# Scaling the output weights a tile ahead, moving the last token tile's transposes and first gather forward, and interleaving the two halves of the last expert unit

## The chip, the cores and the metric

One core of a Trainium2 chip runs the whole kernel. The metric is device microseconds (us) of one execution. Engines are named as the profile names them: PE (TensorE, the matrix engine; PEld is its weight load), DVE (VectorE), ACT (ScalarE), POOL (GpSimd) and SP (SyncE, which issues most DMAs here). Each engine works through its own instructions strictly in the order in which the kernel issues them, and waits on semaphores for the others.

## The reference

One decoder layer over 512 tokens of width 1024, in float32. What matters here:

```python
merged = sigmoid(mg_h) * (o_h @ w_br_hg) + sigmoid(mg_n) * (o_n @ w_br_nsa)
y = (1 + g1) * (merged @ w_out)                 # g1: one scale per output column
x = layer_norm(ALPHA * x + y) * ln1_g + ln1_b
h = layer_norm(x) * (1 + sc2) + sh2
# hierarchical MoE: top group of 4, top 2 of its 8 experts, SwiGLU experts of width 512
y = (1 + g2) * sum over 2 experts of  weight * ((silu(h @ w1) * (h @ w3)) @ w2)
x = layer_norm(ALPHA * x + y) * ln2_g + ln2_b
```

The kernel's units cover all 32 experts whatever the routing, so all of `exp_w1`, `exp_w3` and `exp_w2` is read.

## The kernel before

Tokens lie in NT = 4 tiles of 128. A float32 product is made of three faster ones: an operand is split into a rounded part (`wh`, ACT, L274) and the rest (`wl`, DVE, L275), and three matmuls of the fp32r type are summed. SBUF holds a pool Q of 36 buffers of 128x1024 and a pool S of 24 of 128x512, PSUM a pool of 8 banks. A buffer that is asked for again waits until the last reader of its former content is done.

**Projections.** `Block` holds one block of weight columns: `fetch1` loads a tile of it, `split1` splits a tile. `run_jobs` goes through a list of jobs; after every few matmuls a job yields, and `ahead` then splits one more tile of the blocks to come: first those of the next block, then those of blocks marked `early`. Only the two blocks `wo` (the halves of `w_out`, four tiles of 128x1024 each) are early, and for these `split1` first multiplies the tile by 1 + g1 on DVE (L273). So for each `wo` tile the order is: L273 on DVE, `wh` on ACT, `wl` on DVE. These eight tiles are split during the last jobs of the branch projections (`br_job` with MGN, PSUM tile `pbr`), between DVE's own work of those jobs (L1084, L1088, ACT L1090, DVE L1091: gate, add, and split of the merged rows) and the plain splits of the next branch block (two tiles per block, L274 and L275).

**Output projection, layer norm, routing.** For each token tile i, `out_piece` multiplies the merged rows by `wo` (PSUM `pyo`) and adds x into `z`; `ln` then does the layer norm, the router's logits, the choice of experts, and the row's place within its expert. Tiles 0 to 2 are woven into the matmuls of the next tile; for the last tile `ln` runs by itself. In it DVE makes the statistics and the norm (L1198 to L1205) while PE transposes z (`tail_logits`, PSUM `pzT`; ACT copies it to `zT`) and multiplies it by the router's weights (`plg`, twice: L187, L1218). DVE then chooses the experts (L1223 to L1253, which ends in the mask `mb`), PE runs `gather_first([0, 1])` (a one-hot gather of the rows of tiles 0 and 1 that go to the first four experts, into four banks `pgx`, 32 matmuls), then counts earlier tokens with `mb` (`prk`, L1260 to L1262), then `gather_first([2])`. DVE turns the counts into slots and a one-hot (L1266 to L1275) and splits the last tile (L1277). `gather_first([3])` ends the gather, L1354 and L1356 write it to `xe`, and the first expert unit begins (PSUM `p`).

**Expert units.** 13 units of 128 token slots follow, for 2, 1, 2 or 4 experts at a time; `up` makes the SwiGLU (PSUM `p`), `down` the product with `exp_w2` (`py`) and `combine` adds its rows to the tokens (`pcb`, L1561). With four experts each has 32 slots and its matmuls use 32 of PE's 128 columns, so four run side by side. `load_unit` issues the weights on SP (L1306) in tiles of 512 KB, always as soon as a Q buffer comes free.

**The last unit** is written out (L1671 to L1770). `half_up(h)` makes one half of the output columns, `weighted_halves` scales and splits it (`y`, `yh`, `yl`), `half_add` adds the rows of one token tile (`pcb`, L1707, with their sums), `squares` (ACT, L1689) sums squares about the first half's mean `nsh` (L1721). The rows of `ln2_g` and `ln2_b` are spread over the partitions by 8 matmuls (`pl2`, in the profile `pl`, L1727) and four ACT copies (L1728). Order before: half 0 on PE, `y`; then the split of the two `ln2` rows (L1714 to L1718); the four `half_add`; `nsh`; the 8 `pl2` with their copies; the four `squares`; half 1 on PE; `y` of half 1; the loop for overflow (no block here, but its control flow), then the adds of half 1, the statistics and the output. The weights of half 1 are the last eight tiles that SP loads (L1303).

Of the kernel before, what the change touches and what calls it, by code (L numbers as in the profile page):

```python
# [26 lines left out]
AF = mybir.ActivationFunctionType  # L27
OP = mybir.AluOpType
# [3 lines left out]
NT = T // 128  # L32
# [107 lines left out]
def hybrid_kernel(ctx, tc, a, out, dbg=None, stop=None):  # L140
# [20 lines left out]
    def PS(name):  # L161
        return pp.tile([128, 512], F32, name=name, tag="ps", bufs=8)
# [61 lines left out]
    def layer_stats(src, pre, st=None, later=False):  # L224
        if st is None:
            st = small(pre + "st", 12)
            for q in range(2):
                V.bn_stats(st[:, q * 6:(q + 1) * 6], src[:, q * 512:(q + 1) * 512])
        mv = small(pre + "mv", 2, bufs=4 if pre == "l0" else 2)
        V.bn_aggr(mv, st.rearrange("p (q s) -> p q s", s=6))  # L230
        rs = small(pre + "rs", 2, bufs=4 if pre == "l0" else 2)
        A.activation(rs[:, 0:1], mv[:, 1:2], AF.Ln, bias=eps[:, 0:1])
        A.activation(rs[:, 0:1], rs[:, 0:1], AF.Exp, scale=-0.5)
        if not later:
            V.scalar_tensor_tensor(rs[:, 1:2], mv[:, 0:1], -1.0, rs[:, 0:1], op0=OP.mult, op1=OP.mult)
        return mv, rs
# [13 lines left out]
    class Block:  # L250
        def __init__(self, view, c0, n=256, kt=KT, raw=False, early=False):
            self.view, self.c0, self.n, self.kt, self.raw, self.early = view, c0, n, kt, raw, early
            self.kp = {128: 8, 256: 4, 280: 2, 512: 2}[n]
            self.np = kt // self.kp
            self.w, self.h, self.l = [], [], []

        def fetch1(self):
            kp, n, j = self.kp, self.n, len(self.w)
# [4 lines left out]
        def fetch(self):  # L263
            while len(self.w) < self.np:
                self.fetch1()

        def split1(self, sub=None):
            kp, n, j = self.kp, self.n, len(self.h)
            wh = Q("wh", F32R)[:, :kp * n].rearrange("p (k n) -> p k n", k=kp)
            wl = Q("wl", F32R)[:, :kp * n].rearrange("p (k n) -> p k n", k=kp)  # L270
            if self.early:

                V.tensor_mul(self.w[j], self.w[j], g1b[:, None, self.c0:self.c0 + n].to_broadcast([128, kp, n]))  # L273
            A.activation(wh, self.w[j], AF.Copy)  # L274
            (sub or V).tensor_sub(wl, self.w[j], wh.bitcast(F32))  # L275
            self.h.append(wh)
            self.l.append(wl)
# [30 lines left out]
    g1b = None  # L308
# [313 lines left out]
    for f in range(4):  # L622
        t = S("kcT")
# [535 lines left out]
    def gather_first(tiles, ks=range(8)):  # L1159


        if not pgx0:
            pgx0.extend(PS("pgx").rearrange("p (k s) -> p k s", k=2) for _ in range(4))
        end = tiles[-1] == NT - 1
        for part in ((xhh,), (xhl,)) if end else ((xhh, xhl),):
            for k in ks:
                for i in tiles:
                    for x in part:
                        mm(pgx0[k // 2][:, k % 2, :], x[i][:, k * 128:(k + 1) * 128], hots0[i // 2][:, i % 2, :],
                           i == 0 and x is xhh and k % 2 == 0, end and x is xhl and k % 2 == 1)  # L1170
# [21 lines left out]

    def ln(i, z, st):
        last = i == NT - 1
        mv, rs = layer_stats(z, "l1", st, later=True)
        ac = Q("acc")
        acc.append(ac)
        V.scalar_tensor_tensor(ac, z, mv[:, 0:1], l1g, op0=OP.subtract, op1=OP.mult)  # L1198
        if last:
            plg, lgT = tail_logits()  # L1200
        st = small("l2st", 12)
        for half in range(2):
            s_ = slice(half * 512, (half + 1) * 512)
# [48 lines left out]
        V.scalar_tensor_tensor(mb[:, i, :], iota[:, 0:32], ef[:, 1, i:i + 1], oh2[:, 0, i, :], op0=OP.is_equal, op1=OP.add)  # L1252
        V.tensor_scalar(oh2[:, 1, i, :], iota[:, 0:32], ef[:, 1, i:i + 1], None, op0=OP.is_equal)  # L1253
        if last:
            gather_first([0, 1])
        else:
            yield LN_R

# [74 lines left out]

    W.drain()

    def tail_logits():
        i = NT - 1
        zT[i] = []
        for k4 in range(2):
            pt = z_transposed(i, zs[i], k4 * 4, 4)  # L1340
            t = S("zT")
            A.activation(t, pt, AF.Copy)
            zT[i].append(t)
        return logits_of(i)
    for _ in ln(NT - 1, zs[NT - 1], l1st[NT - 1]):
        pass
    load_unit((0, 1), 8, 12, w_first)
# [340 lines left out]
    def squares(i, h):  # L1688
        A.activation(sq, acc[i][:, halves_[h]], AF.Square, bias=nsh[:, i:i + 1], accum_out=sqs[:, i, h:h + 1])  # L1689

    def half_up(h):

        py = PS("py")
        m = 128 // len(w_now["exp_w2"])
        for k in range(4):
            for x, w in enumerate(w_now["exp_w2"]):
                mm(py[m * x:m * x + m, :], aT[:, k, m * x:m * x + m], w[2 * h + k // 2][:, k % 2 * 512:k % 2 * 512 + 512],
                   k == 0, k == 3, pos=(0, m * x) if m < 128 else None)
        return py

    def half_add(h, y, i):

# [4 lines left out]
        V.tensor_tensor_reduce(out=z, in0=z, in1=pc_, scale=1.0, scalar=0.0, op0=OP.add, op1=OP.add,  # L1707
                               accum_out=sums[:, i, h:h + 1])

    py = half_up(0)  # L1710
    y = weighted_halves(py, cs_, 0, 512)

    oner = Q("oner", F32R)[0:1, 0:128]
    A.activation(oner, ones[0:1, :], AF.Copy)  # L1714
# [1 line left out]
    for t, h_, l_ in zip(l2r, l2h, l2l):  # L1716
        A.activation(h_, t, AF.Copy)
        V.tensor_sub(l_, t, h_.bitcast(F32))  # L1718
    for i in range(NT):
        half_add(0, y, i)  # L1720
    V.tensor_scalar(nsh, sums[:, :, 0], -1.0 / 512, None, op0=OP.mult)  # L1721
    l2g, l2b = Q("l2g"), Q("l2b")
    for t, h_, l_ in zip((l2g, l2b), l2h, l2l):
        for s_ in halves_:
            ps = PS("pl2")
            for j, x in enumerate((h_, l_)):
                mm(ps, oner, x[:, s_], j == 0, j == 1)  # L1727
            A.activation(t[:, s_], ps, AF.Copy)  # L1728
    for i in range(NT):
        squares(i, 0)  # L1730
    py = half_up(1)
    y = weighted_halves(py, cs_, 512, 512)
    overflow()
    A.preload_act_table_set("natural_log_exp_and_others")
    for i in range(NT):
# [61 lines left out]
```

## Time and profile before

| | us |
|---|---|
| median of 3 runs | 1262.7 (1262.7, 1264.41, 1262.7) |
| the profiled execution | 1262.44 |
| its span, first to last instruction | 1260.7 |
| mean granted TensorE clock | 0.978 |
| busy: PE / DVE / ACT / POOL | 1174.7 / 691.6 / 431.3 / 82.8 |
| HBM read | 292.73 MB |

The span is 1.74 us shorter than the execution's time. Busy shares are averages over stages that differ: through the first 600 us PE is busy without a break, from 770 us on the DMA engines are. So what a part of the change is worth is read in its own stage: the branch projections (620 to 690 us), the last tile's routing (744 to 764 us) and the last unit (1222 us to the end).

### The profile page before, as it was taken

How to read it: one execution, taken by the hardware profiler on the slowest of the kernel's cores; microseconds unless marked ns; L12 is line 12 of the kernel's file. 1: busy time of each engine (PE TensorE's matmuls, PEld its weight loads, DVE VectorE, ACT ScalarE, POOL GpSimd, SP SyncE). 2: the span in 40 equal slices, each digit the busy share in tenths (PEclk: the TensorE clock that was granted, in tenths of full speed). 3: DMA queues.
4: the chain of work that ended last, by engine and by line, in shares of the span. 5: the costliest groups of instructions: out<-in, count | busy, mean ns of one | idle time of the engine just before them, and what ended most of it. 6: DMA issues, size and time to landing. Idle time of an engine off the chain costs nothing. (4 is left out here: it accounts for less than half of the span.)

```text
span 1260.7 us, 18162 instructions
## 1 busy us (share of the span) xinstructions
PE 1174.7 (93%) x6455; PEld 805.9 (64%) x6455; DVE 691.6 (55%) x1626; ACT 431.3 (34%) x904; POOL 82.8 (7%) x164
## 2 busy tenths in 40 slices
PE   5999999999999999999987979999999899999976
PEld 4788898778888888878765764434436235455322
DVE  5564988777566656323575687634235124445314
ACT  4333666664445363554232242200102002122014
POOL 3011111101101011002000020000000000000000
PEclk8999999999999999999998989999999999999997
DMA  9954323224234243326334189999999999999991
GB/s 325 299 145 150 106 66 119 85 95 144 88 126 122 75 151 117 100 92 198 105 113 147 54 292 340 409 409 409 408 409 409 409 409 408 406 406 403 409 366 71
DMA packets 137629, 296.10 MB, mean 235 GB/s; under 512 B 11195, under 2 KB 74883, under 8 KB 137536
## 3 DMA queue, kind: packets, MB, share of 16 engines
q1 hardware_dynamic: 128224, 268.57, 58.1%
q0 software_dynamic: 8544, 23.97, 6.1%
q10 hardware_dynamic: 768, 2.37, 0.6%
q8 instruction: 52, 0.85, 0.3%
q14 instruction: 41, 0.34, 0.1%
HBM read 292.73 MB, written 4.76 MB: 236 GB/s over the span
## 5 line engine op out<-in xcount | busy, mean ns | idle before, releaser
L182 PE MATMUL p<-ew,xe 128*32 128x512 f32 (+1 forms) x960 | 195.4, 597 | 11.4 <-DMA ew<-in_exp_w_dram 11.0
L275 DVE TENSOR_TENSOR wl<-wst,wh 128x1024 fp32r<-128x1024 f32 (+1 forms) x93 | 109.5, 1200 | 84.5 <-ACT wh L274 83.8
L182 PEld LDWEIGHTS p<-ew,xe 128*32 128x32 f32 (+1 forms) x960 | 53.2, 122 | 146.9 <-issue 83.1
L274 ACT ACTIVATE wh<-wst 128x1024 fp32r<-128x1024 f32 (+1 forms) x94 | 93.6, 1031 | 44.8 <-DVE wst L273 32.1
L1512 DVE TENSOR_TENSOR s<-s,p 128x512 f32<-128x512 f32 x13 | 8.9, 688 | 176.6 <-PE p L182 160.9
L182 PE MATMUL py<-ew,aT 128*32 128x512 f32 (+1 forms) x464 | 96.4, 598 | 8.7 <-DMA ew<-in_exp_w_dram 5.8
L182 PEld LDWEIGHTS py<-ew,aT 128*32 128x32 f32 (+1 forms) x464 | 24.7, 121 | 73.2 <-issue 36.5
L1520 ACT ACTIVATE aT<-pat 128x512 f32<-128x512 f32 x13 | 7.8, 597 | 177.4 <-PE pat L186 177.4
L1561 DVE TENSOR_TENSOR acc<-acc,pcb 128x512 f32<-128x512 f32 x96 | 58.3, 678 | 7.9 <-PE pcb L180 7.9
L1535 ACT ACTIVATE yh<-y 128x512 fp32r<-128x512 f32 x26 | 16.4, 630 | 132.3 <-DVE y L1533 130.8
L180 PE MATMUL pgx<-pm,xhh 128*128 128x256 f32 (+1 forms) x224 | 56.3, 295 | 0.0
L180 PE MATMUL pgx<-pm,xhl 128*128 128x256 f32 (+1 forms) x224 | 55.0, 290 | 0.0
L1533 DVE SCALAR_TENSOR_TENSOR y<-py,cs,g2b 128x512 f32<-128x512 f32 x26 | 19.4, 748 | 62.2 <-PE py L182 62.0
L180 PE MATMUL pmg<-hh,wh 128*128 128x512 f32 x128 | 50.4, 394 | 0.0
L180 PE MATMUL psg<-hh,wh 128*128 128x512 f32 x128 | 50.3, 393 | 0.0
L180 PE MATMUL psg<-hl,wh 128*128 128x512 f32 x128 | 49.9, 390 | 0.0
L180 PE MATMUL psg<-hh,wl 128*128 128x512 f32 x128 | 49.9, 390 | 0.0
L180 PE MATMUL pmg<-hh,wl 128*128 128x512 f32 x128 | 49.8, 389 | 0.0
L180 PE MATMUL pmg<-hl,wh 128*128 128x512 f32 x128 | 49.8, 389 | 0.0
L180 PE MATMUL pcb<-yh,pT 128*128 128x512 f32 x104 | 43.6, 420 | 6.6 <-issue 5.1
L513 POOL DMA_DIRECT2D adaw<-in_ada_w_dram x64 | 34.6, 542 | 196.5 <-PE ptp L186 44.8
L180 PEld LDWEIGHTS pgx<-pm,xhh 128*128 128x128 f32 x224 | 44.2, 200 | 3.2 <-issue 2.3
(538 smaller groups left out, 2788.1 us busy)
## 6 DMA issues: line engine op xcount, KB each, us to landing
ew<-in_exp_w_dram SPq DMA_DIRECT2D x380, 512.0 KB, 10.1
wst<-in_w_in_dram SPq DMA_DIRECT2D x66, 512.0 KB, 4.9
adaw<-in_ada_w_dram POOLq DMA_DIRECT2D x64, 256.0 KB, 3.1
adaw<-in_ada_w_dram SPq DMA_DIRECT2D x16, 512.0 KB, 9.2
wst<-in_w_br_hg_dram SPq DMA_DIRECT2D x8, 512.0 KB, 5.5
wst<-in_w_br_nsa_dram SPq DMA_DIRECT2D x8, 512.0 KB, 3.6
wst<-in_w_out_dram SPq DMA_DIRECT2D x8, 512.0 KB, 6.5
ext_d<-ext_d POOLq DMA_DIRECT2D x1, 2560.0 KB, 17.2
```

Source lines behind the costliest of these rows:

```text
L180: PE.matmul(o, l, r, start=start, stop=stop)
L182: PE.matmul(o, l, r, start=start, stop=stop, tile_position=pos)
L274: A.activation(wh, self.w[j], AF.Copy)
L275: (sub or V).tensor_sub(wl, self.w[j], wh.bitcast(F32))
L513: P_.dma_start(w, ada[:, k, 2048 + j * 512:2560 + j * 512])
L1512: V.tensor_mul(s1, s1, p3)
L1520: A.activation(aT, at_.rearrange("p (f s) -> p f s", f=4), AF.Copy)
L1533: V.scalar_tensor_tensor(y, py, cs_, g2b[c0 // 512][:, c0 % 512:c0 % 512 + n], op0=OP.mult, op1=OP.mult)
L1535: A.activation(yh, y, AF.Copy)
L1561: V.tensor_add(acc[i][:, s_], acc[i][:, s_], pc_)
```

## The change

Three edits. (1) `Block.scale(j)` is the former multiplication by 1 + g1; `split1` for tile j issues it for tile j + 1 too, between `wh` on ACT and `wl` on DVE. It does so only for tiles that have been fetched, and all four of a block are. (2) In `ln` of the last tile, the transposes and copies of z (`tail_transposed`) and `gather_first([0])` are issued first; the logits follow where they were, and after the choice of experts only `gather_first([1])` runs before the counts. (3) In the last unit, the split of the `ln2` rows comes ahead of half 0; the 8 `pl2` matmuls follow half 0 on PE at once, their copies follow the first `yh` on ACT; then the first inner index of half 1 is issued expert by expert, each of the four matmuls followed by one `half_add` of half 0; then the second index, `nsh`, the other two indices, and after them the four `squares` and `y` of half 1.

```diff
+        def scale(self, j):
+            if self.early and self.scaled <= j < len(self.w):
+                V.tensor_mul(self.w[j], self.w[j],
+                             g1b[:, None, self.c0:self.c0 + self.n].to_broadcast([128, self.kp, self.n]))
+                self.scaled = j + 1
         def split1(self, sub=None):
...
-            if self.early:
-                V.tensor_mul(self.w[j], self.w[j], g1b[:, None, self.c0:self.c0 + n].to_broadcast([128, kp, n]))
+            self.scale(j)
             A.activation(wh, self.w[j], AF.Copy)
+            self.scale(j + 1)
             (sub or V).tensor_sub(wl, self.w[j], wh.bitcast(F32))
...
     def ln(i, z, st):
         last = i == NT - 1
+        if last:
+            tail_transposed()
+            gather_first([0])
         mv, rs = layer_stats(z, "l1", st, later=True)
...
         if last:
-            plg, lgT = tail_logits()
+            plg, lgT = logits_of(i)
...
         if last:
-            gather_first([0, 1])
+            gather_first([1])
...
-    def half_up(h):
-        py = PS("py")
+    def half_up(h, py, ks):
         m = 128 // len(w_now["exp_w2"])
-        for k in range(4):
+        for k in ks:
             for x, w in enumerate(w_now["exp_w2"]):
                 mm(py[m * x:m * x + m, :], aT[:, k, m * x:m * x + m], w[2 * h + k // 2][:, k % 2 * 512:k % 2 * 512 + 512],
                    k == 0, k == 3, pos=(0, m * x) if m < 128 else None)
-        return py
+                yield
...
-    py = half_up(0)
-    y = weighted_halves(py, cs_, 0, 512)
     oner = Q("oner", F32R)[0:1, 0:128]
...
-    for i in range(NT):
-        half_add(0, y, i)
-    V.tensor_scalar(nsh, sums[:, :, 0], -1.0 / 512, None, op0=OP.mult)
+    py, py1 = PS("py"), PS("py")
+    for _ in half_up(0, py, range(4)):
+        pass
     l2g, l2b = Q("l2g"), Q("l2b")
-    for t, h_, l_ in zip((l2g, l2b), l2h, l2l):
+    pls = []
+    for h_, l_ in zip(l2h, l2l):
         for s_ in halves_:
             ps = PS("pl2")
             for j, x in enumerate((h_, l_)):
                 mm(ps, oner, x[:, s_], j == 0, j == 1)
-            A.activation(t[:, s_], ps, AF.Copy)
+            pls.append(ps)
+    y = weighted_halves(py, cs_, 0, 512)
+    for j, ps in enumerate(pls):
+        A.activation((l2g, l2b)[j // 2][:, halves_[j % 2]], ps, AF.Copy)
+    for x, _ in enumerate(half_up(1, py1, (0, 1))):
+        if x < NT:
+            half_add(0, y, x)
+    V.tensor_scalar(nsh, sums[:, :, 0], -1.0 / 512, None, op0=OP.mult)
+    for _ in half_up(1, py1, (2, 3)):
+        pass
     for i in range(NT):
         squares(i, 0)
-    py = half_up(1)
-    y = weighted_halves(py, cs_, 512, 512)
+    y = weighted_halves(py1, cs_, 512, 512)
     overflow()
```

## Rows read from the trace of the kernel before

**Rows 1.** Busy time by stretch, core 0: us, then busy us and instructions of PE, PEld, DVE, ACT, POOL, the granted PE clock, the DMA share and GB/s.

```profile
730.00:762.00 32.00, 25.29 (x176) 23.02 (x175) 27.38 (x81) 13.59 (x21) 6.79 (x6) 0.79 0.93 340
762.00:767.00 5.00, 5.00 (x32) 2.53 (x32) 3.87 (x18) 3.53 (x7) 0.00 (x0) 1.00 0.53 137
...
772.00:1226.00 454.00, 427.97 (x2147) 187.46 (x2143) 180.66 (x419) 62.50 (x126) 1.01 (x2) 1.00 1.03 407
```

**Rows 2.** Waits of the SP queue before it could issue a weight tile, first from 756 to 764 us, then from 764 to 772 us: what it waited for, us in total, times, longest.

```profile
SPq L1306 <- DVE xhl L1277: 9.6, 1, 9.6
...
SPq L1306 <- PE p L182: 5.5, 4, 2.9
```

**Rows 3.** Timeline of DVE and ACT, 630 to 676 us: start, us, engine, line, operation, tiles, and in brackets the idle time before it and what ended it. The lines from 641.67 on begin the repeats of the same pattern.

```profile
631.86 1.22 DVE L273 TENSOR_TENSOR wst<-wst,g1b 128x1024 f32<-128x1024 f32 x1
633.17 1.06 ACT L274 ACTIVATE wh<-wst 128x1024 fp32r<-128x1024 f32 x1 [15.55 <-DVE wst L273]
634.27 1.22 DVE L275 TENSOR_TENSOR wl<-wst,wh 128x1024 fp32r<-128x1024 f32 x1 [1.19 <-ACT wh L274]
...
638.96 0.68 DVE L1084 TENSOR_TENSOR sgm<-sgm,pbr 128x512 f32<-128x512 f32 x1
...
641.67 1.22 DVE L273 TENSOR_TENSOR wst<-wst,g1b 128x1024 f32<-128x1024 f32 x1
...
651.81 2.36 DVE L275 TENSOR_TENSOR wl<-wst,wh 128x1024 fp32r<-128x1024 f32 x2 [0.25 <-ACT wh L274]
...
674.03 2.36 DVE L275 TENSOR_TENSOR wl<-wst,wh 128x1024 fp32r<-128x1024 f32 x2 [0.26 <-ACT wh L274]
```

**Rows 4.** Group of DVE instructions of one line from 629 to 674.5 us: count, busy us, mean ns of one, idle us just before them and what ended it.

```profile
L275 DVE TENSOR_TENSOR wl<-wst,wh 128x1024 fp32r<-128x1024 f32 x13 | 15.7, 1223 | 10.0 <-ACT wh L274 10.0
```

**Rows 5.** Timeline of PE in the same stretch: the two places where it stood idle for longer, and the last matmul ahead of the second.

```profile
651.84 0.62 PE L180 MATMUL pbr<-onh,wh 128*128 128x512 f32 x1 [3.64 <-ACT wh L274]
...
664.54 0.39 PE L180 MATMUL pbr<-onh,wl 128*128 128x512 f32 x1
674.05 0.80 PE L180 MATMUL pbr<-onh,wh 128*128 128x512 f32 x1 [9.12 <-ACT wh L274]
```

**Rows 6.** SP's timeline: the last of the eight loads of `w_out`, and the sixteen loads of the last unit's `exp_w2` (from the first issue to the end of the last). Then the page's groups of DMA issues: count, KB each, median us from issue to landing.

```profile
645.28 0.37 SPq L260 DMA_DIRECT2D wst<-in_w_out_dram  x1
...
1202.04 20.98 SPq L1303 DMA_DIRECT2D ew<-in_exp_w_dram  x16
...
ew<-in_exp_w_dram SPq DMA_DIRECT2D x380, 512.0 KB, 10.1
...
wst<-in_w_out_dram SPq DMA_DIRECT2D x8, 512.0 KB, 6.5
```

**Rows 7.** Timeline of the last token tile's routing, PE and DVE: columns as in Rows 3. The first line is the count of the tile before, the last one the first matmuls of the first expert unit.

```profile
744.34 0.19 PE L180 MATMUL prk<-pk 128*128 128x32 bf16 x1 [2.11 <-DVE pk L1252]
...
749.54 1.97 PE L182 MATMUL plg<-zT,pk 128*64 128x128 f32 x16 [2.76 <-ACT zT L1342]
...
752.34 0.56 PE L180 MATMUL pgx<-pm,xhh 128*128 128x256 f32 x1
...
752.89 0.20 DVE L1223 SCALAR_TENSOR_TENSOR pk<-wsh,l1mv,plg 128x36 f32<-128x36 f32 x1
...
756.39 0.25 DVE L1252 SCALAR_TENSOR_TENSOR pk<-cst,ef,pk 128x32 bf16<-128x32 f32 x1
...
758.69 0.27 PE L180 MATMUL prk<-pk 128*128 128x32 bf16 x4
...
759.00 0.22 DVE L1266 TENSOR_TENSOR t<-pk,prk 128x64 f32<-128x64 f32 x1 [2.21 <-PE prk L180]
...
763.29 13.95 PE L182 MATMUL p<-ew,xe 128*64 128x512 f32 x64
```

**Rows 8.** Timeline of the last two units, PE, DVE and ACT: columns as in Rows 3. An f32 matmul of a quarter of the columns (128*32) makes two records, one for each of its passes; the `x8` and `x10` lines are merged records of experts side by side. The first three lines show PE going from such matmuls to `pcb`, in the unit before the last.

```profile
1190.45 1.90 PE L182 MATMUL p<-ew,xe 128*32 128x512 f32 x10 [0.23 <-DMA ew<-in_exp_w_dram]
1192.29 0.50 PE L180 MATMUL pcb<-yh,pT 128*128 128x512 f32 x1
1192.63 0.39 PE L180 MATMUL pcb<-yl,pT 128*128 128x512 f32 x1
...
1222.50 1.90 PE L182 MATMUL py<-ew,aT 128*32 128x512 f32 x10 [0.98 <-DMA ew<-in_exp_w_dram]
...
1228.45 0.49 PE L180 MATMUL pl<-l2gh,oner 1*128 1x512 f32 x1
...
1230.18 0.38 PE L180 MATMUL pl<-l2bl,oner 1*128 1x512 f32 x1
1230.49 1.06 PE L182 MATMUL py<-ew,aT 128*32 128x512 f32 x8
...
1231.14 0.67 DVE L1707 CUSTOM_DVE_ANT_0 acc<-acc,pcb 128x512 f32<-128x512 f32 x1
...
1232.06 0.72 ACT L1689 ACTIVATE sq<-acc,nsh 128x512 f32<-128x512 f32 x1 [0.78 <-DVE nsh L1721]
...
1233.05 1.90 PE L182 MATMUL py<-ew,aT 128*32 128x512 f32 x10
...
1234.60 0.72 ACT L1689 ACTIVATE sq<-acc,nsh 128x512 f32<-128x512 f32 x1
...
1235.78 0.63 ACT L1535 ACTIVATE yh<-y 128x512 fp32r<-128x512 f32 x1 [0.36 <-DVE y L1533]
```

More of the change, by code (lines that the diff above doesn't have):

```diff
@@ L254, in __init__ @@
             self.np = kt // self.kp
-            self.w, self.h, self.l = [], [], []
+            self.w, self.h, self.l, self.scaled = [], [], [], 0
         def fetch1(self):
@@ L1334, in hybrid_kernel, with tail_transposed @@
     W.drain()
-    def tail_logits():
+    def tail_transposed():
         i = NT - 1
@@ L1343, in tail_logits @@
             zT[i].append(t)
-        return logits_of(i)
     for _ in ln(NT - 1, zs[NT - 1], l1st[NT - 1]):
```

## The prediction

> **What bounds the kernel now.** I read the stretches first, then the waits of the DMA queue, then the timeline of each of the three places that the diff touches. From 772 to 1226 us the DMA engines are busy throughout, at 407 GB/s [rows 1]: the expert weights stream, and PE waits for them. Nothing in the compute of that stage sets its length; what counts is when the stream starts. From 762 to 767 us it still has a hole (DMA share 0.53), and before that it is on and off [rows 1]. The reader is to see what ends the hole: SP holds each weight tile back until an SBUF buffer comes free. It waits 9.6 us for the split of the last token tile (L1277) and then for the first unit's matmuls `p` [rows 2]. So the stream hangs on the compute before it, and compute that finishes earlier there moves the whole stream and the end with it. At the end the last weight tile lands, PE makes half 1 from it, and everything after is a chain.
>
> **Part 1, the output weights.** In the stretch 630 to 674 us DVE is the bound, not PE: PE stands idle 3.64 and 9.12 us, both until ACT has split the next branch block [rows 5], and ACT gets to that only behind L1090, which waits for L1088 at the end of DVE's backlog. For each `wo` tile DVE multiplies, then stands 1.19 us until ACT has rounded, then subtracts [rows 3]; the thirteen L275 of the stretch have 10.0 us of idle ahead of them, of which 0.51 belongs to the two pairs of plain splits [rows 3, 4], so the eight `wo` tiles have 9.5 us. One instruction that waits for nothing takes 1.14 us from start to start (2.36 less 1.22) [rows 3]. Two `wo` tiles take 7.10 us now (631.86 to 638.96) and 4 x 1.14 = 4.56 us without waits: 2.54 us less, four times, 10.2 us. The next tile's multiplication fills the wait. Left are the first and the last tile of a block, where ACT ends 2.41 us after the multiplication starts (634.27 less 631.86) and DVE has 2.28 us of work by then: 0.13 us, four times. Sum **10.2 - 0.5 = 9.6 us**. Every wait that the moved multiplication adds: it needs its tile from DRAM and, being ahead of L1084, L1091 and the plain splits on DVE, would hold them, ACT's L1090 behind them and PE behind that. The last `w_out` tile is issued at 645.28 and takes 6.5 us in the median [rows 6]: about 652. Its multiplication, now in the group before 667 us, moves to about 658, so 6 us are spare.
>
> What is late next? PE resumes at 674.05 now and would at 664.4. The block before ends at 664.9 now [rows 5]; without the first stall of 3.64 us, and without the slow start behind it, it ends near 659. So PE still waits 5 us for DVE, and the whole 9.6 us reach it. From there to 744 us no row waits for anything but the engines themselves, so I let all of it move along. PE's clock after the stall may fall for longer or shorter than now: 0.9 us either way, half of what a few microseconds at half rate would cost.
>
> **Part 2, the last token tile.** The masks `mb` start at 756.39 and last 0.25 us, but PE counts with them only at 758.69, since the 32 gather matmuls from 752.34 on are ahead of it; DVE stands idle 2.21 us for that, until 759.00 [rows 7]. The change takes 16 of the 32 out of that place and puts them where PE stands idle 2.76 us before 749.54 [rows 7]. With 16 left from about 752.9 at 0.2 us each (32 took 752.34 to 758.69), PE is done at 756.2, before the mask, and DVE goes on at 757.0: **2.0 us** earlier, and L1277 and `p` with it, which are exactly what SP waits for [rows 2]. The hole has 0.47 x 5 = 2.4 us of idle DMA before 767 us [rows 1], so 2.0 us fit. Against it: the moved 16 take some 3.4 us at this pace where 2.76 are idle, so the logits come about 0.7 us later and DVE's L1223, at 752.89 some 0.4 us after its operand, about 0.3 us later. I take **1.7 us**. On ACT only two copies move ahead of two tiny ones, in idle time. None of the three edits issues or moves a DMA, so the queues of SP and POOL keep their order.
>
> **Part 3, the last unit.** Half 1's last ten records start at 1233.05 [rows 8]. SP's last load ends its issue at 1223.02, and 10.1 us is the median to landing [rows 6]: 1233.1. So half 1 cannot end sooner, however early it begins, and the gain is nothing. The cost: four experts side by side make a pass of 0.42 us together (ten records, four passes, 1.90 us; eight records, two passes, 1.06) [rows 8]. Interleaved with `pcb`, which takes all columns, each expert pays its two passes alone. Half 0's last pass starts at 1222.50 + 3 x 0.43 = 1223.8; the step from such a pass to a full matmul is 0.52 (1190.45 + 3 x 0.43 to 1192.29), so `pl2` begins at 1224.3. Its eight and the step back take 2.04 us (1228.45 to 1230.49) [rows 8], so expert 0 begins at 1226.4. Each expert then costs 0.43 + 0.52 + 0.34 (first to second `pcb`, 1192.29 to 1192.63) + 0.31 (1230.18 to 1230.49) = 1.60 us [rows 8]. The fourth `pcb` pair has its second matmul at 1226.4 + 3 x 1.60 + 1.29 = 1232.5, its add on DVE at about 1232.9 where it is now at 1231.14. The first `squares` follows an add by 0.92 us (1231.14 to 1232.06), the four are 0.85 us apart (1232.06 to 1234.60) [rows 8]: 1233.8 to 1237.2. `yh` of half 1 stands behind them on ACT; it starts at 1235.78 now, 0.36 us after the squares [rows 8]. PE itself ends half 1 about 0.6 us later (six passes from 1232.8), which the squares cover. So **1.4 us lost**. Between 0 (the experts overlap with `pcb` after all) and 2.5 us (twice the step cost).
>
> A rule that speaks against this part: the Trainium skill, TensorEngine Tiling (Array Packing), Tiling Modes, says that a change of the tiling mode, not merely of the tile, drains TensorE. The trace agrees in part, with starts 0.52 and 0.31 us apart at a change. If each change waited for the whole record to end (0.62 and 0.39 us), the eight changes would cost 0.7 us more, and the sum would be 0.7 us higher.
>
> **The sum.** 9.6 + 1.7 - 1.4 = 9.9 us. The profiled execution took 1262.44 us (span 1260.7 and 1.74 around it), so 1252.5; the median of the three runs is 0.3 us above it: **1252.8 us**.
>
> **The rivals.** (a) Part 2 loses the clock. PE fell to half rate around 744 us after 2.11 us of idling [rows 7], and the mean over 730 to 762 is 0.79 [rows 1]. The change leaves PE with up to 3 us of nothing just before the counts, in front of the last 32 gather matmuls. At the 0.2 us each of now (mostly half rate) they take 6.4 us; at full rate half of that, so 3 us hang on it, and the first unit would start at half rate too. Part 2 then gives from +0.5 to -1.8 us instead of 1.7: 1254 to 1256.3, I say 1255.5. For it: the idle time is real. Against it: now the same place follows a low clock and PE is fuller before. The Trainium skill, TensorE: Matmul & The Clock Gate (HAM oscillation — how this bites in real kernels), says that PE, idling between bursts while it waits for data, drops to half rate and starts the next burst cold; by that rule this rival is what happens. The trace shows both: a slow first matmul after 3.64 us of idling (0.62 us against 0.39) [rows 5], and a clock of 1.00 through all the waits for weights [rows 1]. (b) Part 3 costs nothing, because PE overlaps passes of one expert with `pcb`: 1251.4. No row shows such overlap. (c) Part 1's time is not passed on, because the stream is fixed by something that part 1 doesn't move: parts 2 and 3 alone, 1262.5. Against it: every wait of SP that I read is for compute [rows 2]. (d) **Slower**: the multiplication of the second block's last tile, moved ahead, waits for its load on DVE, with L1084, the plain splits and PE's next block behind it. It decides from a landing 9.8 us after the planned 658, at about 668: each microsecond past that is one more than now. That would be if SP had to give that tile a buffer which PE frees only with the block that ends at 664.9 now [rows 5]: landing 671.4, 671.4 - 658 - 9.6 = 3.8 us lost in part 1, and 1266.2 in all. Against it: in the trace it is issued at 645.28 [rows 6], and an earlier release can only help. (e) The change doesn't do what it says, because the next tile isn't fetched when `scale` looks: then part 1 is nothing, as in (c). But all four loads of a block are issued before its first split.
>
> **How the numbers follow.** Forecast, 1250 to 1254: 0.60. (a) 0.22, (b) 0.10, (c) and (e) 0.05, (d) 0.03. The low end is 9.6 + 0.9 + 2.0 - 0 = 12.5 us: 1250.2. The high end takes in the worst of (a) and of part 1's clock: 9.6 - 0.9 - 1.8 - 1.4 = 5.5 us: 1257.2. Measurement tells 0.2% (2.5 us) from no change: faster by more than that holds in the forecast, (a) and (b), 0.92; within it (c) and (e), 0.05; slower (d), 0.03.
>
> **What would show it.** Right: no idle of 1.19 us ahead of L275 for `wo` tiles but for about 0.13; PE resuming its last branch block some 9.6 us sooner after a stall of about 5 us; the count `prk` right behind the mask, L1266 without its 2.21 us; the weight stream 11 us earlier with the same GB/s; in the last unit `pcb` pairs 1.6 us apart, and `yh` of half 1 behind `squares` rather than behind `y`. Wrong: buffers of the weight stream released by something else than `p` and L1277, a DMA hole as long as before, or PE's clock at half rate from the counts into the first unit.

## The result and the profile after

| | us |
|---|---|
| median of 4 runs, before | 1263.22 (1262.7 to 1264.41) |
| median of 4 runs, after | 1253.95 (1251.85 to 1256.47) |
| ratio | 0.9926, 95% interval 0.9903 to 0.9949 |
| profiled execution, after | 1251.85 (span 1250.1, mean granted clock 0.986) |

That is 9.3 us faster; 1252.8 us was predicted. The four runs after lie 4.6 us apart, those before 1.7. Now and then an execution of any kernel takes far longer (1316 to 3872 us on record); such executions are left out of all medians and ratios here.

**The branch projections.** Timeline of the changed kernel, DVE, then PE, columns as in Rows 3; below it the group of the subtractions from 629 to 674.5 us, columns as in Rows 4. L270 is now the scaling, L279 `wh`, L281 `wl`.

```profile
632.11 2.36 DVE L270 TENSOR_TENSOR wst<-wst,g1b 128x1024 f32<-128x1024 f32 x2
...
647.25 2.36 DVE L281 TENSOR_TENSOR wl<-wst,wh 128x1024 fp32r<-128x1024 f32 x2 [0.26 <-ACT wh L279]
...
658.96 0.39 PE L180 MATMUL pbr<-onh,wl 128*128 128x512 f32 x1
664.67 0.80 PE L180 MATMUL pbr<-onh,wh 128*128 128x512 f32 x1 [5.32 <-ACT wh L279]
...
665.93 0.80 PE L180 MATMUL pbr<-onh,wl 128*128 128x512 f32 x1
...
668.58 0.40 PE L180 MATMUL pbr<-onh,wl 128*128 128x512 f32 x1
```

```profile
L281 DVE TENSOR_TENSOR wl<-wst,wh 128x1024 fp32r<-128x1024 f32 x14 | 16.8, 1221 | 0.7 <-ACT wh L279 0.5
```

Two scalings stand back to back, the subtractions have 0.7 us of idle ahead of them for 10.0 [rows 4], and PE has one stall of 5.32 us for the two of 3.64 and 9.12 [rows 5]. It resumes 9.38 us sooner. It still resumes slowly: from the first matmul to the ninth it is 3.91 us (664.67 to 668.58), eight steps where those that follow take 0.23 us each.

**The routing.** Timeline of the last token tile, PE and DVE; below it busy time by stretch, columns as in Rows 1.

```profile
734.74 1.16 PE L186 MATMUL pzT<-cst,z 128*128 128x128 f32 x8 [0.30 <-DVE z L1126]
735.66 0.36 PE L180 MATMUL pgx<-pm,xhh 128*128 128x256 f32 x1
...
737.73 1.09 PE L182 MATMUL plg<-zT,pk 128*64 128x128 f32 x16
...
741.44 0.24 PE L180 MATMUL prk<-pk 128*128 128x32 bf16 x3
746.35 0.25 DVE L1261 SCALAR_TENSOR_TENSOR pk<-cst,ef,pk 128x32 bf16<-128x32 f32 x1
746.65 0.19 PE L180 MATMUL prk<-pk 128*128 128x32 bf16 x1 [4.97 <-DVE pk L1261]
746.88 0.22 DVE L1275 TENSOR_TENSOR t<-pk,prk 128x64 f32<-128x64 f32 x1
747.04 0.41 PE L180 MATMUL pgx<-pm,xhl 128*128 128x256 f32 x1
747.25 0.41 PE L180 MATMUL pgx<-pm,xhh 128*128 128x256 f32 x1
748.65 1.22 DVE L1286 TENSOR_TENSOR xhl<-xh,xhh 128x1024 fp32r<-128x1024 f32 x1
752.41 13.95 PE L182 MATMUL p<-ew,xe 128*64 128x512 f32 x64
```

```profile
740.00:745.00 5.00, 1.68 (x17) 1.56 (x16) 4.50 (x15) 1.78 (x3) 0.00 (x0) 0.86 1.04 397
745.00:750.00 5.00, 3.35 (x16) 3.35 (x16) 4.36 (x17) 2.84 (x3) 0.00 (x0) 0.50 1.01 407
```

In the kernel before, `xhl` stood here:

```profile
760.76 1.22 DVE L1277 TENSOR_TENSOR xhl<-xh,xhh 128x1024 fp32r<-128x1024 f32 x1
```

The slots (L1275) follow the mask at once; the 2.21 us of idle before them are gone [rows 7]. From the mask to `xhl` it is 2.30 us, for 4.37 before (756.39 to 760.76). But PE stood idle for 4.97 us, the granted clock is 0.50 from 745 to 750 us (the lower of its two levels, 1.2 of 2.4 GHz), and the first 16 of the 32 gather matmuls behind it start 0.21 us apart. `p` begins 3.76 us after `xhl`, for 2.53 before (760.76 to 763.29): 752.41, that is 6.06 us after the mask instead of 6.90.

**The last unit.** Timeline, PE, DVE and ACT, columns as in Rows 8.

```profile
1211.26 1.90 PE L182 MATMUL py<-ew,aT 128*32 128x512 f32 x10 [0.99 <-DMA ew<-in_exp_w_dram]
...
1215.12 1.04 PE L182 MATMUL py<-ew,aT 128*32 128x512 f32 x2
1216.10 0.50 PE L180 MATMUL pcb<-yh,pT 128*128 128x512 f32 x1
1216.44 0.40 PE L180 MATMUL pcb<-yl,pT 128*128 128x512 f32 x1
1216.76 1.04 PE L182 MATMUL py<-ew,aT 128*32 128x512 f32 x2
...
1221.68 2.78 PE L182 MATMUL py<-ew,aT 128*32 128x512 f32 x24
...
1224.53 0.75 DVE L1541 SCALAR_TENSOR_TENSOR y<-py,cs,g2b 128x512 f32<-128x512 f32 x1 [1.84 <-PE py L182]
1225.26 0.72 ACT L1697 ACTIVATE sq<-acc,nsh 128x512 f32<-128x512 f32 x1
1225.98 0.61 ACT L1543 ACTIVATE yh<-y 128x512 fp32r<-128x512 f32 x1
1227.27 0.06 DVE L1576 MEMSET ocnt<- 128x1 f32 x1
1229.77 0.79 PE L180 MATMUL pcb<-yh,pT 128*128 128x512 f32 x1 [5.31 <-issue]
```

The stream is 11.24 us earlier at the last records of half 0 (1211.26 for 1222.50 [rows 8]). `pcb` pairs come 1.64 us apart, and `yh` of half 1 stands behind the last of the squares (L1697): 14.72 us after those records, for 13.28 before.

### The profile page after: what moved, and what is told of

The parts are those of the page before. It is cut to its first block, busy times and chain, and to the rows that moved or that the text cites. A ratio compares the mean times of both kernels' runs of the same rounds, so it can differ in the third digit from the quotient of the medians.

```text
span 1250.1 us, 18158 instructions
## 1 busy us (share of the span) xinstructions
PE 1171.4 (94%) x6455; PEld 803.1 (64%) x6455; DVE 691.8 (55%) x1626; ACT 431.5 (35%) x904; POOL 85.4 (7%) x164
## 5 line engine op out<-in xcount | busy, mean ns | idle before, releaser
L182 PE MATMUL p<-ew,xe 128*32 128x512 f32 (+1 forms) x960 | 195.6, 597 | 10.6 <-DMA ew<-in_exp_w_dram 10.1
L281 DVE TENSOR_TENSOR wl<-wst,wh 128x1024 fp32r<-128x1024 f32 (+1 forms) x93 | 109.6, 1201 | 75.4 <-ACT wh L279 74.5
L182 PE MATMUL py<-ew,aT 128*32 128x512 f32 (+1 forms) x464 | 99.1, 598 | 8.8 <-DMA ew<-in_exp_w_dram 5.9
L279 ACT ACTIVATE wh<-wst 128x1024 fp32r<-128x1024 f32 (+1 forms) x94 | 93.9, 1031 | 32.7 <-DVE wst L270 20.2
```

The costliest lines, as they stand in the source:

```text
L182: PE.matmul(o, l, r, start=start, stop=stop, tile_position=pos)
```

## The experiments

Each is timed beside the kernel before on the same chip; `us` is the median. Differences of 1 us are smaller than what the times tell apart (of the kernels built on the changed one, only e8 and e11 have an interval clear of its 0.9903 to 0.9949), so the small terms are read from each run's timeline, as distances within it.

| run | us | ratio to before, 95% interval |
|---|---|---|
| e1, part 1 alone | 1253.70 | 0.9923 (0.9909 to 0.9937) |
| e2, part 2 alone | 1262.33 | 0.9998 (0.9986 to 1.0011) |
| e3, part 3 alone | 1264.24 | 1.0010 (1.0000 to 1.0020) |
| e4, parts 1 and 2 | 1252.78 | 0.9922 (0.9904 to 0.9941) |
| e5, changed, routing filled | 1251.10 | 0.9902 (0.9889 to 0.9916) |
| e6, changed, squares behind the loop | 1252.87 | 0.9930 (0.9912 to 0.9948) |
| e7, changed, adds first | 1253.51 | 0.9922 (0.9907 to 0.9937) |
| e8, changed, no scaling | 1245.27 | 0.9860 (0.9844 to 0.9877) |
| e9, parts 1 and 2, routing filled | 1250.80 | 0.9895 (0.9881 to 0.9910) |
| e10, changed, stall filled | 1250.98 | 0.9899 (0.9883 to 0.9915) |
| e11, parts 1 and 2, both filled | 1245.81 | 0.9866 (0.9850 to 0.9881) |
| e12, changed, PE's list longer | 1251.29 | 0.9912 (0.9896 to 0.9928) |

The routing in each, in us from the start of the mask (before L1252, after L1261):

| | before | e1 | after | e2 | e4 | e5 | e9 | e10 | e11 | e12 |
|---|---|---|---|---|---|---|---|---|---|---|
| to `xhl` | 4.37 | 3.97 | 2.30 | 2.29 | 2.29 | 2.29 | 2.29 | 2.30 | 2.47 | 2.29 |
| `xhl` to `p` | 2.53 | 2.52 | 3.76 | 3.63 | 4.00 | 2.53 | 2.52 | 4.71 | 2.53 | 3.99 |
| to `p` | 6.90 | 6.49 | 6.06 | 5.92 | 6.29 | 4.82 | 4.81 | 7.01 | 5.00 | 6.28 |

The last unit in each, in us from the last ten records of half 0, without those that repeat a column and without e5 and e9, whose clock fell there (in e7 it fell too, but PE still reached the last ten records of half 1 early and waited, 10.55 us behind those of half 0 as in the kernel before):

| | before | after | e3 | e4 | e6 | e7 | e10 | e11 | e12 |
|---|---|---|---|---|---|---|---|---|---|
| `y` of half 1 | 12.49 | 13.27 | 13.26 | 12.49 | 13.27 | 12.49 | 13.25 | 12.50 | 13.25 |
| its `yh` | 13.28 | 14.72 | 14.71 | 13.28 | 14.41 | 13.27 | 14.71 | 13.29 | 14.70 |
| memset of the loop | 14.58 | 16.01 | 16.00 | 14.58 | 15.71 | 14.58 | 15.99 | 14.59 | 15.99 |
| `pcb` of half 1 | 17.57 | 18.51 | 18.81 | 17.59 | 18.29 | 17.53 | 16.57 | 15.15 | 16.56 |

**Each part by itself.** In e1 to e3 one of the three hunks stands in the kernel before; in e4 the third is taken out of the changed kernel.

> The kernel before with the scaling a tile ahead and nothing else. My account: 9.4 to 9.6 us faster than before, as predicted for this part, because PE's last branch block resumes 9.4 us sooner (664.67 after, 674.05 before) and everything up to the routing moves along; the first unit's p starts near 753.7. Rival, the gain of the whole change is smaller than the sum of its parts because the weight stream takes up only some of it: clearly under 9 us, with p early but the last half-0 records of the last unit no more than 8 us early. Rival (c) of the prediction, nothing is passed on: same time as before.

> The kernel before with only the last tile's transposes and first gather led. My account: DVE's part is done 2.0 us sooner (the slots L1266 start near 757.0 instead of 759.00, xhl near 758.7 instead of 760.76), but PE's idle time of some 5 us ahead of the count leaves its clock low, the last 32 gather matmuls run 0.21 us apart, and p starts only 0.8 us sooner (near 762.5): 0.8 to 1.2 us faster in all. Rival, the prediction as it stood: p sooner by 1.7 us and the time too. Rival (a) at its worst: up to 0.5 us slower.

> The kernel before with only the last unit rewritten. My account: half 0 on PE ends where it did (last records at 1222.5), the yh of half 1 starts 1.4 us later, behind the four squares (near 1237.2 instead of 1235.78), and the time is 0.6 to 1.4 us longer. Rival (b), it costs nothing: yh at 1235.8 and the same time. Rival, it gains because the eight pl2 and half 1 begin earlier: y of half 1 before 1234.99 and the time shorter.

> The changed kernel with the last unit put back as it was before; parts 1 and 2 stay. My account: 0.6 to 1.4 us faster than the changed kernel, that is 10.2 to 12.0 us faster than before; yh of half 1 follows y by 0.8 us and the last half-0 records by 13.3 us as before, where the changed kernel has 14.7. Rival (b), part 3 costs nothing: the time of the changed kernel.

Part 1 alone gives 9.1 us by the medians and 9.7 by the ratio, the whole change within the noise; rival (c) of the prediction falls: its `p` is at 752.87 and its last half-0 records at 1211.95, 10.4 and 10.6 us sooner. Part 2 alone gives 0.4 us (0.3 by the ratio) with an interval on both sides of nothing. Part 3 alone costs 1.5 us (1.3 by the ratio, with an interval from nothing to 2.5), and e4 without it is 0.5 us (by the ratios) to 1.2 us (by the medians) faster than the changed kernel, which the times do not tell apart. The timeline of e2 (PE and DVE) shows where part 2 went:

```profile
756.76 0.25 DVE L1255 SCALAR_TENSOR_TENSOR pk<-cst,ef,pk 128x32 bf16<-128x32 f32 x1
757.06 0.18 PE L180 MATMUL prk<-pk 128*128 128x32 bf16 x1 [3.64 <-DVE pk L1255]
...
758.24 0.28 PE L180 MATMUL pgx<-pm,xhl 128*128 128x256 f32 x1
758.36 0.38 PE L180 MATMUL pgx<-pm,xhh 128*128 128x256 f32 x1
758.53 0.42 PE L180 MATMUL pgx<-pm,xhl 128*128 128x256 f32 x1
758.74 0.42 PE L180 MATMUL pgx<-pm,xhh 128*128 128x256 f32 x1
...
759.05 1.22 DVE L1280 TENSOR_TENSOR xhl<-xh,xhh 128x1024 fp32r<-128x1024 f32 x1
762.68 13.95 PE L182 MATMUL p<-ew,xe 128*64 128x512 f32 x64
```

After 3.64 us of idling PE starts the gather at 0.12 us from start to start and falls to 0.21 in the middle of it. `xhl` is 2.1 us nearer to the mask than before, `p` only 1.0.

**Is it the clock?** e5 gives PE work in the idle time ahead of the count:

```diff
         if last:
             gather_first([1])
+            pf = PS("pfill")
+            for q in range(32):
+                PE.matmul(pf[:, 0:256], xhh[1][:, q % 8 * 128:(q % 8 + 1) * 128], hots0[0][:, 1, :], start=True, stop=True)
```

> The changed kernel with 32 matmuls of 128x256 added on PE between the last tile's second gather (tile 1) and the count by its mask. They write a PSUM tile that nobody reads; the result is the same, PE only has work for some 4 of its 5 us of idle time ahead of the count. My account: part 2 gives 0.3 us instead of 1.7 because PE idles there, its clock falls to 0.50, and the last 32 gather matmuls run 0.21 us apart instead of 0.12. With the filling the clock stays at 1.00 through 750, xhl stays where it is in the changed kernel (748.65), and p starts 1.3 us sooner (near 751.1 instead of 752.41): about 1.3 us faster than the changed kernel. Rival, the clock falls all the same: the added matmuls take 0.21 us each, the count waits for them until about 748, and p starts 1 to 2 us later. Rival, p is held by something else (the weights or xe): the clock stays up and p stays at 752.4.

Timeline of e5, PE and DVE, and its busy time by stretch, columns as in Rows 1:

```profile
744.21 4.00 PE L1267 MATMUL pfill<-pm,xhh 128*128 128x256 f32 x32
748.05 0.28 PE L180 MATMUL prk<-pk 128*128 128x32 bf16 x4
750.14 1.22 DVE L1289 TENSOR_TENSOR xhl<-xh,xhh 128x1024 fp32r<-128x1024 f32 x1
752.67 13.95 PE L182 MATMUL p<-ew,xe 128*64 128x512 f32 x64
```

```profile
745.00:750.00 5.00, 5.00 (x46) 4.96 (x46) 4.31 (x23) 4.25 (x3) 0.00 (x0) 1.00 1.00 369
```

The clock is 1.00 where it was 0.50, the mask is still counted at once, and from `xhl` to `p` it is 2.53 us again: 1.23 us won back, as expected. (`p` itself is not at 751.1, because this execution ran 1.5 us late up to the mask.) The second table splits without exception: 2.52 or 2.53 where PE was busy ahead of the count, 3.63 to 4.71 where it stood. The three kernels with the gap that are not in it fit too (3.85 in e6, 3.64 in e7, 3.40 in e8); over all eight the gap is 2.25 to 4.98 us. The Trainium skill, TensorE: Matmul & The Clock Gate (HAM oscillation — how this bites in real kernels), has PE start cold after it idled for data; here six of the eight start the gather 0.21 us apart, while e2 (3.64 us idle) and e7 (2.25) start it 0.12 apart and fall to 0.21 within it. But the time of e5 is 3.0 us below the changed kernel's by the ratios, more than the 1.23; e12 deals with the rest.

**What part 3 costs, and by what.** e6 moves the four `squares(i, 0)` behind the overflow loop; e7 leaves everything of part 3 but the interleaving:

```diff
-    for x, _ in enumerate(half_up(1, py1, (0, 1))):
-        if x < NT:
-            half_add(0, y, x)
+    for x in range(NT):
+        half_add(0, y, x)
+    for _ in half_up(1, py1, (0, 1)):
+        pass
```

> The changed kernel with the four squares of half 0 moved on ACT from ahead of the yh of half 1 to behind the overflow loop. My account: part 3 costs what it does because yh stands behind the squares (0.7 us) and because y itself is 0.8 us later. So yh now follows y by 0.8 us (near 1225.3 for 1225.98), the loop's memset and pcb come 0.7 us sooner, the squares of half 1 end up to 0.9 us later on ACT but still ahead of the instruction that needs them: 0.7 us faster than the changed kernel. Rival, the entry into the loop is set by PE or SP and not by yl: pcb stays 18.5 us behind the last half-0 records and the time is the same. Rival, the squares behind the loop hold the statistics: up to 1 us slower.

> The changed kernel with the four half_add of half 0 all ahead of half 1 instead of one after each expert's matmul; the ln2 rows and pl2 stay early. My account: the loss of part 3 is the alternation of quarter-column and full matmuls (1.64 us for each expert). Without it nsh is done near 1219, the squares end before the weights of half 1 have landed, y follows the last half-0 records by 12.5 us and yh by 13.3 as without part 3: 0.7 to 1.4 us faster than the changed kernel. Rival, the loss is in the early pl2 and not in the alternation: yh 14.7 us behind the last half-0 records as in the changed kernel.

e7 puts `y` and `yh` back at 12.49 and 13.27 us: the loss is the alternation, not the early `pl2`. e6 missed: `yh` follows `y` by 1.14 us, not 0.8, since it starts 0.39 us after `y` has ended although nothing stands ahead of it on ACT. Why is open. It won 0.31 us at `yh` and 0.22 at `pcb`, which the times can't show. So of the 1.44 us by which part 3 delays `yh`, 0.78 is the later `y`, and 0.31 goes away when the squares do.

**What the stall costs.** e8 leaves out the multiplications by 1 + g1. e10 fills PE's stall ahead of the last branch block:

```diff
                 ft = ft0 + j
+                if off == MGN and ft == 6:
+                    pf = PS("pfill")
+                    for q in range(20):
+                        PE.matmul(pf, onh(0)[:, 0:128], onh(0), start=True, stop=True)
                 ps = PS("pbr")
```

> The changed kernel without the eight multiplications by 1 + g1 (their effect on the output is left out). They take 1.14 us each on DVE, 9.1 us. My account: DVE is still the bound in the branch projections, PE stands 5.32 us at its last branch block; without the multiplications this stall goes to nothing and PE itself is the bound, so 5 to 5.5 us faster than the changed kernel and no more. Rival, DVE is no longer the bound after part 1 and the stall has another cause (the landing of that block's weights, or ACT): under 2 us. Rival, DVE bounds all the way: 9 us.

> The changed kernel with 20 matmuls of 128x512 added on PE ahead of the last branch block, where PE stands 5.32 us; they write a PSUM tile that nobody reads. My account: the stall costs more than its idle time, because the clock then falls (0.66 and 0.65 from 660 to 670 us) and the first nine matmuls take 3.91 us instead of 2.04. Filled, PE still resumes with ACT's wh (664.67) but at full clock, and everything behind it to the first unit's p comes 1.9 us sooner: 1.9 us faster than the changed kernel. It also tells why the kernel without the multiplications gained 7.4 us in its profiled run where the stall is 5.32. Rival, the slow start is not from the idle time (weights' loads, PSUM): the first matmuls stay 0.43 to 0.63 us apart and the time is the same.

My account of e8 was too small: 8.3 us faster than the changed kernel by the ratios, 7.35 at `p` (745.06) and 6.96 at the first `pyo` behind the branch blocks (670.69 for 677.65). Its PE has no idle time over 1 us from 640 to 690 us and a clock of 1.00 from 650 to 690. So the stall cost more than its 5.32 us: the eight steps behind it take 3.91 us where 1.8 are usual, 2.1 us more. (It is 6.96 and not the sum because e8's block before ends 0.6 us later.) e10 shows how much of that is the clock (PE's timeline):

```profile
660.11 4.70 PE L1090 MATMUL pfill<-onh 128*128 128x512 f32 x20
665.60 0.50 PE L180 MATMUL pbr<-onh,wh 128*128 128x512 f32 x1 [0.79 <-ACT wh L279]
665.93 0.40 PE L180 MATMUL pbr<-onl,wh 128*128 128x512 f32 x1
666.86 0.50 PE L180 MATMUL pbr<-onh,wl 128*128 128x512 f32 x1 [0.53 <-DVE wl L281]
...
668.35 0.39 PE L180 MATMUL pbr<-onh,wl 128*128 128x512 f32 x1
```

PE resumes at full clock. But the third matmul needs DVE's next subtraction, and so it does in the changed kernel, whose weight load waits for it too:

```profile
665.93 0.29 PEld L180 LDWEIGHTS pbr<-onh,wl 128*128 128x128 f32 x1 [0.76 <-DVE wl L281]
```

In both it starts 1.26 us behind the first (664.67 to 665.93, 665.60 to 666.86), so that part of the slow start is not the clock. From the third to the ninth it is 1.49 us instead of 2.65. These 1.16 us are what the clock costs here, and not the 1.9 of my account: up to the mask e10 gains 1.19 (80.49 us from resuming, for 81.68). The routing then loses 0.95 of it again: although PE stands only 3.41 us ahead of the count, for 4.97, `p` came 7.01 us after the mask. At `p` the filling has won 0.24 us; e10's 3.4 us by the ratios are mostly something else, see e12.

**Together.** e9 is e4 with the filling of e5, e11 is that with the filling of e10.

> Parts 1 and 2 with the 32 filling matmuls ahead of the count, and the last unit as it was before (part 3 undone). My account: part 1 as measured alone (9 to 9.6), part 2 with the clock kept up (2.0), nothing lost in the last unit: 11 to 12 us faster than before; xhl to p 2.5 us, y of half 1 12.5 us and its yh 13.3 us behind the last half-0 records. Rival, the filled kernel was fast for another reason (the run with part 3 had 12.4 us): then the filling brings nothing without part 3, and this is 10 us faster than before.

> Parts 1 and 2, both fillings, the last unit as before. My account: the sum of the two runs beside it: 13 to 14 us faster than before. Rival, the gains do not add up, because an earlier p only makes SP wait for buffers or the stream start into a fuller DMA: 11 to 12 us.

e11 is the fastest of the kernels that leave nothing out: 17.5 us below the kernel before, more than the 13 to 14 expected, and, by the ratios, 7.6 below the changed one. Its profiled execution is 7.4 us shorter than the changed kernel's: 3.5 ahead of the last unit, 1.4 without part 3, 1.9 at the entry into the loop, 0.5 behind it. e9 gave 12.5 for 11 to 12. Both times have the shorter entry into the loop in them, which neither expectation had, so what the filling brings to e9 is read from `xhl` to `p` (2.52 us for 4.00 in e4) and not from its time. In e9's profiled execution the last unit ran into a clock of 0.50, and its half 1 took 6.34 us instead of 4.46, so its last unit is not in the table.

**The rest of it.** In the four kernels with filling PE's first `pcb` follows the memset ahead of the overflow loop 2 to 3 us sooner than in all others. e12 tries that alone:

```diff
+        if n == 8:
+            pf = PS("pfill")
+            for q in range(32):
+                PE.matmul(pf[:, 0:32], onesb, onesb[:, 0:32], start=True, stop=True)
         act = up(xe, (n % 2) * 128, ws, mid=between if last or inside else None)
```

> The changed kernel with 32 small matmuls (bf16, 128x32, into a PSUM tile that nobody reads) put into the stage where PE waits for weights, ahead of the ninth expert unit. They do nothing for the clock in the routing and cost no time there; they only make PE's instruction list longer. Observation: in the four kernels with filling matmuls pcb follows the loop's memset by 0.6 us, in all others by 2.5 to 3.5, and the trace shows a 16 KB transfer on the instruction queue in front of it (1229.18 in the changed kernel, pcb at 1229.77; already at 1227.6 in the first filled one). My account: where such a transfer falls depends on how long PE's list is, and about 2 us of what the filled kernels gained are from that and not from the clock. Then this kernel has the memset-to-pcb step at 0.6 us, p at the place of the changed kernel, and is 1.5 to 2 us faster than it. Rival, the short step comes from the earlier filling itself (the clock, the earlier stream): the step stays at 2.5 us or more and the time is that of the changed kernel.

First the DMA view of the changed kernel from 1228 to 1230.5 us (busy tenths in 40 slices, then packets, MB and share of each queue), then the same of e12, then its timeline:

```profile
DMA  0000000000000030009000000000000000000000
...
q8 instruction: 1, 0.02, 2.3%
q14 instruction: 1, 0.01, 0.8%
```

```profile
DMA  0000000000000400000000000000000000000000
...
q14 instruction: 1, 0.01, 1.2%
```

```profile
1227.48 0.06 DVE L1576 MEMSET ocnt<- 128x1 f32 x1
1228.05 0.50 PE L180 MATMUL pcb<-yh,pT 128*128 128x512 f32 x1 [3.37 <-DVEq L1590]
```

In the changed kernel a transfer on the instruction queue q8 falls between the memset and `pcb`, in slice 19 of 40, so from 1229.1 us on, and PE's wait is put down to "issue". In e12 no such transfer is there, and `pcb` follows the memset by 0.57 us, where the changed kernel has 2.50. Over all the profiles it is the same: in each of the nine kernels without added matmuls one q8 transfer falls between the memset and `pcb`, in none of the five with them. The routing is as in the changed kernel (`xhl` to `p` 3.99 us), and the time is 1.8 us less by the ratios, with intervals that overlap. So about 1.9 us of what e5, e9, e10 and e11 won is this, and not the clock in the routing. In e12 some 0.7 us follow, since PE, after the shorter wait, starts the adds at full clock (0.50 us for the first `pcb`, for 0.79): from the memset to the end it is 20.22 us for 22.83.

## Why the prediction was right, and where it was off

**Part 1 was right in each step.** The idle ahead of the subtractions went from 10.0 to 0.7 us; PE resumed at 664.67 where 664.4 was worked out, after a stall of 5.32 where 5 was; up to the transposes of the last tile 0.69 us came on top, inside the 0.9 allowed for the clock (`pzT` at 734.74, 10.07 us sooner than before, where it began at 744.81). e1 puts the part at 9.1 us (medians) or 9.7 (ratio) for 9.6.

**Part 2 is the term that was mis-sized.** "2.0 us earlier, and L1277 and `p` with it" holds for L1277 (2.07 us nearer to the mask) and fails for `p` (0.84). The step took PE's part behind the count as unchanged, and it took the 16 matmuls left ahead of the count at 0.2 us each, done just ahead of the mask; at full clock they took 0.12 each (739.45 to 741.44), and that made the 4.97 us of idling. Rival (a) had the mechanism, with a hole of up to 3 us and at too high a price: the idle time did lower the clock, and it took 1.23 us of the 2.07. The 0.3 us for late logits did not come either: from `pzT` to the mask it is 11.61 us for 11.58, for the gather ahead of the logits kept the clock up and `plg` took 1.09 us instead of 1.97 [rows 7]; e1, without that gather, stands 3.55 us there and its `plg` takes 1.98. In time the part gives 0.4 us (e2) where 1.7 stood, and 0.43 from the mask to `p` on top of part 1 (6.06 for e1's 6.49).

**Part 3 was right in size and in the main in mechanism.** The step for an expert is 1.64 us (1.60 predicted), `yh` is 1.44 us later behind half 0 (1.4), and e3 is 1.5 us slower than before. The squares, which were to cover the later end of half 1, account for only part of it, as e6 shows. That the landing of the last weights allows no gain is borne out by e7: there PE waits ahead of the last ten records of half 1 (1222.80), until 0.6 us after the traffic of the weights ends (1222.2). How they land was overlooked: from 1218 us on the DMA engines move about 23 GB/s, after some 390 until 1216, so the last unit stands behind a tail of 4 us that no part of the change touches. Its cause is open. Of the 1.44 us, 0.94 reached `pcb` in the profiled execution, because the entry into the loop happened to take 2.50 us for 2.99. Rival (b) falls with e3 and e7. The Trainium skill's rule of a drain at each change of tiling mode (TensorEngine Tiling (Array Packing), Tiling Modes), taken as a wait for the whole record, would have added 0.7 us, 0.18 for each expert; the 1.64 leaves 0.04.

**The sum.** 9.9 us was predicted from one profiled execution. The parts measured alone add up to 9.1 + 0.4 - 1.5 = 8.0 by the medians and 8.7 by the ratios, the change itself to 9.3; the difference is within the 4.6 us by which its own runs differ. Some luck is in the total: 1253.95 lies at the upper edge of the forecast, with two of its four runs beyond 1254. And in the profiled execution, 10.6 us shorter, what part 2 did not bring was made up by terms that the sum had at nothing: 0.69 of a shorter slow start behind part 1, 0.36 in the weight stream, 0.49 at the entry into the loop. The spread of the runs may have its place in what differs between the profiles: the clock in the routing (`xhl` to `p` from 3.40 in e8 to 4.71 in e10 with the same code there), and the clock in the last unit, which fell in e5, e7 and e9 and not in the others. These are single executions of different kernels; what decides it from one execution to the next was not tried. Rivals (c), (d) and (e) did not happen; (d) was not brought about by an experiment, so its price stays an estimate.

## What to carry to other kernels

When work is moved out of the way of a critical instruction, ask what the engine does in the hole that it leaves: here DVE had the slots and the last split 2 us sooner, and PE, idle for 5 us ahead of the count, did the first 16 of the next 32 matmuls at half rate. Price a stall of TensorE as its idle time plus what the clock costs behind it (5.32 + 1.2 us here), and keep that apart from the waits for other engines that stand there anyway. A few matmuls that nobody reads kept the clock up in both such places, but only ahead of the count did the gain (1.23 us) reach `p`; at the stall 0.24 of 1.19 did. Do not alternate matmuls that use part of the columns with ones that use all: an expert's turn with its `pcb` pair took 1.64 us, where such pairs follow each other every 0.47 us in the kernel before and four experts side by side make a pass in 0.43.

## What the runs showed of the hardware that was not expected

How long it takes from DVE's memset ahead of a loop to PE's first matmul behind it changed with matmuls added to PE's list far ahead: 2.50 to 3.46 us in nine kernels, 0.56 to 0.63 in the five with 20 to 52 more matmuls, though the loop ran no turn in any. The profile shows it only as "issue" in front of `pcb` and as a transfer on the queue q8, which carries 52 of them in one execution, 0.85 MB in all. The Trainium skill, Runtime: NRT & Kernel Launch (Instruction fetch mechanics), says that instructions come in blocks and that a taken branch can make an engine wait for one; the trace agrees in that a 16 KB transfer falls there in the nine and in none of the five, and puts the difference at about 2 us here. That it is the place of the block's border in PE's list, and not only its length, was not tried. Nor was the one other thing that the five share, a PSUM tile or two more for the added matmuls; the trace shows no wait for one.
